# The second block's products as pairs of f32 halves on unsplit weights, on one Trainium2 core

## Chip, core and metric

The kernel runs on one core of a Trainium2 chip. The metric is device microseconds of one execution; the time before is the median of three runs. All matmuls run on TensorE (PE), which multiplies 128 rows of stationary weights (loaded by PEld) with up to 512 moving columns and writes to PSUM. VectorE is DVE, ScalarE is ACT, GpSimd is POOL, SyncE is SP. The trace gives one profiled execution, in us from the span's start.

## What is computed

Two transformer blocks on 512 tokens of width 1024, all in float32. The first (attention over tokens and context, then 32 routed experts, twice) is left alone by the change. The second, cut to its products:

```
h = rmsnorm(x, pre_mix_g)
z = h @ w_in                                  # 1024 x 7696
y_gla = gla_branch(...)                       # gated linear attention
y_sc  = sc_b * causal_dwconv(sc_c * sc_x)     # short convolution
y_dil = dilated_branch(d_q, d_k, d_v, pos)    # strided window attention
proj  = einsum('bsgc,gcd->bsgd', [y_gla, y_sc, y_dil], w_branch)
gates = sigmoid(h @ w_gate + b_gate)
x = x + rmsnorm(sum(gates * proj) @ w_mix_out, post_mix_g)
h = rmsnorm(x, pre_ffn_g)
gt = causal_dwconv(h @ w_ff_gate) + ff_conv_b  # 1024 x 2816
x = x + rmsnorm((gelu(gt) * (h @ w_ff_up)) @ w_ff_down, post_ffn_g)
```

## The kernel before

`second` (L1723) makes a plan of 92 weight tiles, nearly all 1 MB, in the order in which they are used, and a `Stream` (L34) loads them from HBM into slots. `ws.get()` splits the next tile: ACT writes `wh`, the weights rounded to fp32r (a reduced f32), and DVE (POOL in a few places) writes the rest, `wl = raw - wh`. The tokens `hTh`/`hTl`, the branch results `yh`/`yl`, `mTh`/`mTl` and `uTh`/`uTl` are split alike by `split` (L232). `mm3` (L226) then makes one product of three fp32r matmuls, high*high, high*low and low*high. Two raw slots are held, with pairs of split tiles behind them.

`proj_T` (L1763) takes a block of 128 weight columns as the stationary operand and moves 512 tokens: 8 products for 1024 rows. `proj` (L1770) takes 128 tokens as the stationary operand and moves 256 weight columns; in `dilated` the tokens of two of three groups are every fourth token. `out_rows` (L1915) takes 128 tokens and moves 512 columns, over 8 blocks of rows for `w_mix_out` and 22 for `w_ff_down`, each for four blocks of tokens and two halves of the width.

`second_body` (L1776) goes through the stages in order: the end of the first block and its norm (`front`, `back`, with `V`), `gla` with `short_conv` as filler, `dilated` with the projections of the next head as filler, gates and branch projections (`pm`, `pb`), the first `out_rows` with the norm of the feed-forward (`then`, which goes over `turned`), gate and up, the second `out_rows`. Within these, small f32 products stand in `gla` (`pg` L2086, `pe` L2063 in fp32r, `po`) and in `dilated` (`s` L2224, `po` L2250). A scheduler sets the order of instructions within a stage; each engine's queue runs in that order.

The experts of the first block, which the change leaves alone, hold products of 64 stationary columns: `up` (L1548) and `down` (L1572) take 64 tokens as weights and send two column ranges of the moving tile into the two halves of the PSUM partitions. The lines that matter there:

```
for i in range(2):
    for k in range(KC):                      # KC = 8
        for n in range(2):
            nc.tensor.matmul(pu[c][i][64 * n:64 * n + 64], xs[:, k, tok], w[:, k % 4, n * 256:(n + 1) * 256], ...)
```

`down` has four k and two n, with 512 columns each.

Of the kernel before, what the change touches and what calls it, by code (L numbers as in the profile page):

```python
# [23 lines left out]
P = 128  # L24
# [146 lines left out]
class Kern:  # L171
# [1542 lines left out]
    def turned(self, n, b, hT, pt):  # L1714

        for k0 in (0, 4):
# [46 lines left out]
    def proj_T(self, w, c, m=P):  # L1763

        pm = self.ps.tile([P, 512], F32, tag="mm", name="pm")
        for k in range(KC):
            self.mm3(pm[:m], w[0][:, k, c:c + m], w[1][:, k, c:c + m], self.hTh[:, k], self.hTl[:, k], k == 0, k == KC - 1)
        return pm

    def proj(self, w, tok, pm, c=0):  # L1770

        n = w[0].shape[2]
        for k in range(KC):
            self.mm3(pm[:, c:c + n], self.hTh[:, k, tok], self.hTl[:, k, tok], w[0][:, k], w[1][:, k], k == 0, k == KC - 1)

    def second_body(self):  # L1776
        nc, tc, A = self.nc, self.tc, self.A
        ws, proj_T = self.ws, self.proj_T
        with ExitStack() as es:
# [4 lines left out]
            self.hTh = hTh = hp.tile([P, KC, 512], FR, tag="hh", name="hTh")  # L1784
            self.hTl = hTl = hp.tile([P, KC, 512], FR, tag="hl", name="hTl")
            V = hp.tile([P, 4, 512], F32, name="V")
            with tc.tile_pool(name="sbx", bufs=2) as xp:
                second = []
                for b in range(4):
# [3 lines left out]
                    if b == 0:  # L1793
# [3 lines left out]
                        nc.gpsimd.dma_start(g, self.bcast_rows(A["pre_mix_g_2"], D))  # L1797
                gb = self.res[:, 4:6]
# [10 lines left out]
                Ws = [ws.get(0, sub=nc.gpsimd) for _ in range(2)]  # L1809

                def back(b, n):
                    self.turned(n, b, (hTh, hTl), lambda: ps.tile([P, 4, P], F32, tag="aux", name="pt"))
# [5 lines left out]
                for _ in piped(4, front, back, 2):  # L1818
                    pass
            self.res_stack.close()  # L1820

            def y_tiles(name):
                pool = ent(tc.tile_pool(name=name, bufs=1, side="right"))
                return tuple(pool.tile([P, 4, 512], FR, name=f"y{x}") for x in "hl")
# [3 lines left out]
            with ExitStack() as fs:  # L1828
                gla = self.gla(V, *y[0], ps)
                next(gla)  # L1830
                sp = fs.enter_context(tc.tile_pool(name="scp", bufs=2, side="right"))
                both(gla, self.short_conv(*y[1], sp))
            y.append(y_tiles("sby2"))
            self.dilated(*y[2], ps)

            mp = ent(tc.tile_pool(name="sbm", bufs=1, side="right"))
            mTh = mp.tile([P, KC, 512], FR, name="mTh")
            mTl = mp.tile([P, KC, 512], FR, name="mTl")
            bg = mp.tile([P, 24], F32, name="bg")
            nc.sync.dma_start(bg, A["b_gate_2"][0].rearrange("(k p) -> p k", p=P))  # L1840
            with tc.tile_pool(name="sbg", bufs=2) as gp:
                for d0 in range(0, 8, 2):
                    acc = gp.tile([P, 2, 512], F32, tag="acc", name="acc")
                    for g in range(3):
                        gts = []
                        wg = ws.get()
# [5 lines left out]
                        wh, wl = ws.get()  # L1852
                        for i in range(2):
                            pb = ps.tile([P, 512], F32, tag="mm", name="pb")
                            d = slice(i * P, (i + 1) * P)
                            for k in range(4):
                                self.mm3(pb, wh[:, k, d], wl[:, k, d], y[g][0][:, k], y[g][1][:, k], k == 0, k == 3)
# [3 lines left out]
                            else:  # L1861
                                nc.vector.tensor_mul(gt, gt, pb)
                                nc.vector.tensor_add(acc[:, i], acc[:, i], gt)
                            if g == 2:
                                self.split(mTh[:, d0 + i], mTl[:, d0 + i], acc[:, i])
# [4 lines left out]
            self.hTh = hTh = hp.tile([P, KC, 512], FR, name="hTh")  # L1870
            self.hTl = hTl = hp.tile([P, KC, 512], FR, name="hTl")
# [4 lines left out]
            with tc.tile_pool(name="sbmx", bufs=2) as xp:  # L1876
# [3 lines left out]
                def then(x, b, pt):  # L1880
                    self.turned(self.rms_apply(x, g, xp), b, (hTh, hTl), pt)

                self.out_rows(lambda k: (mTh[:, k], mTl[:, k]), KC, "post_mix_g_2", self.x_d, xp, then)
        with ExitStack() as es:
            ent = es.enter_context
            up = ent(tc.tile_pool(name="sfu", bufs=1, side="right"))
            uTh = up.tile([P, 22, 512], FR, name="uTh")
            uTl = up.tile([P, 22, 512], FR, name="uTl")
            with h2, tc.tile_pool(name="sfps", bufs=4, space=PSUM) as self.ps:
                with tc.tile_pool(name="sfg", bufs=2) as gp:  # L1890
                    for c0 in range(0, 22, 2):
                        ts = []
                        wg = ws.get(sub=None if c0 else nc.gpsimd)
# [12 lines left out]
                        wu = ws.get()  # L1906
                        for i in range(2):
                            t = ts[i]
                            pu = proj_T(wu, i * P)
                            nc.vector.tensor_mul(t, t, pu)  # L1910
                            self.split(uTh[:, c0 + i], uTl[:, c0 + i], t)
            with tc.tile_pool(name="sfx", bufs=2) as xp:
                self.out_rows(lambda k: (uTh[:, k], uTl[:, k]), 22, "post_ffn_g_2", A["out"], xp)

    def out_rows(self, lhs, kc, gname, dst, xp, then=None):  # L1915
# [6 lines left out]
        with tc.tile_pool(name="orps", bufs=1, space=PSUM) as ps:  # L1922
            pm = [ps.tile([P, 2, 512], F32, name=f"acc{b}", tag=f"acc{b}") for b in range(4)]

            def block(b, k0, w):
                tok = slice(b * P, (b + 1) * P)
                for i in range(2):
                    k = k0 + i
                    h, l = lhs(k)
                    for n in range(2):  # L1930
                        c = slice(n * 512, (n + 1) * 512)
                        self.mm3(pm[b][:, n], h[:, tok], l[:, tok], w[0][:, i, c], w[1][:, i, c], k == 0, k == kc - 1)

            for k0 in range(0, kc - 4, 2):
                w = self.ws.get()
                for b in range(4):
                    block(b, k0, w)
            w = [self.ws.get(), self.ws.get(ahead=0)]
            for b in range(4):
# [9 lines left out]
                if then and b:  # L1949
                    self.after(then, x, b - 1, ps)  # L1950
            if then:
# [6 lines left out]
    def short_conv(self, yTh, yTl, sp):  # L1958
# [5 lines left out]
        for i0 in (0, 2):  # L1964
            us, ts = [], []
            wb = ws.get()
# [5 lines left out]
            wc = ws.get()  # L1972
# [6 lines left out]
            wx = ws.get()  # L1979
            for i in range(2):  # L1980
# [7 lines left out]
                nc.vector.tensor_mul(t, t, v)  # L1988
                self.split(yTh[:, i0 + i], yTl[:, i0 + i], t)
                yield  # L1990

    def token_major(self, out, func, ps):

        for n in range(2):
            w = self.ws.get()
# [6 lines left out]
    def gla(self, V, yTh, yTl, ps):  # L2002
# [3 lines left out]
        with ExitStack() as es:  # L2006
# [4 lines left out]
            M = gp.tile([P, 9, P], FR, name="M")  # L2011
            mf = gp.tile([P, 9, P], F32, tag="mf", name="mf")
            nc.sync.dma_start(mf, A["k_gla_m"])
            nc.scalar.activation(M, mf, AF.Copy)
            mask = gp.tile([P, 8, P], F32, tag="mf", name="mask")
# [11 lines left out]
            for i in range(4):  # L2027
                if i % 2 == 0:
                    w = ws.get()
                nc.scalar.activation(qkT[:, i], proj_T(w, i % 2 * P), AF.Copy, scale=0.125 if i < 2 else 1.0)  # L2030
            aT = gp.tile([16, 512], F32, name="aT")
            nc.scalar.activation(aT, proj_T(ws.get(), 0, m=16)[:16], AF.Copy)

            lah = gp.tile([P, 4, 256], FR, name="lah")
# [323 lines left out]
```

## Time and profile before

| | |
|---|---|
| median of three runs | 3473.0 us (3469.5 to 3478.71) |
| the profiled execution | 3476.67 us, span 3474.9 us |
| PE busy | 3146.0 us (91%), 19045 instructions |
| PEld busy | 2289.0 us (66%) |
| DVE, ACT, POOL busy | 1479.0, 1038.0, 546.3 us |
| second block, from its first transposes | about 2285 to 3475 us |

Busy time counts the union of a group's rows, and a matmul's row includes its way through the array, so rows of one group overlap. The cost of a matmul in a stream is the distance between starts. Two of the experts' stages (about 660 to 1200 and 1800 to 2230 us) are the places where DMA is full.

### The profile page before, as it was taken

The page shows a single profiled execution, that of the slowest core. Times are in us where ns is not written, and L with a number is a line of the kernel's source. Part 1 is how long each engine was busy: PE and PEld are TensorE (multiplying, and loading weights), DVE is VectorE, ACT ScalarE, POOL GpSimd, SP SyncE. Part 2 cuts the span into 40 slices and gives each one's busy share as a digit, 9 for nine tenths or more (in the row PEclk, how much of TensorE's full clock was granted, in tenths as well). Part 3 has the DMA queues.
Part 4 walks back from the last instruction along what each step waited for, and adds up shares of the span by engine and source line. Part 5 has one row for each costly group of instructions (what it writes and reads, how often), then busy time and mean ns, then how long its engine had stood idle before and what let it go on. Part 6 is the DMA issues. An engine that isn't in the chain of part 4 may idle for free. (4 is left out here: it accounts for less than half of the span.)

```text
span 3474.9 us, 50552 instructions
## 1 busy us (share of the span) xinstructions
PE 3146.0 (91%) x19045; PEld 2289.0 (66%) x19045; DVE 1479.0 (43%) x3317; ACT 1038.0 (30%) x2243; POOL 546.3 (16%) x533
## 2 busy tenths in 40 slices
PE   7999999799999938999799999569999999979998
PEld 3677767555555526887655555258798888858887
DVE  5578665521111147655622112154533333365533
ACT  4355562111111114655211111023223332233321
POOL 1101002141211111011232121220022210010000
PEclk9999999799999978999899999879999999989999
DMA  7433142699999641111499999552121212423332
GB/s 249 153 98 108 53 155 98 278 398 416 416 416 415 274 135 49 30 54 55 168 381 366 399 416 402 230 157 73 54 75 49 67 55 91 148 77 97 97 127 73
DMA packets 273506, 647.72 MB, mean 186 GB/s; under 512 B 58210, under 2 KB 176370, under 8 KB 223042
## 3 DMA queue, kind: packets, MB, share of 16 engines
q1 hardware_dynamic: 245522, 602.04, 46.5%
q0 software_dynamic: 26608, 38.36, 3.6%
q8 instruction: 187, 3.06, 0.4%
q10 hardware_dynamic: 1088, 3.42, 0.3%
q14 instruction: 101, 0.83, 0.1%
HBM read 670.51 MB, written 47.61 MB: 207 GB/s over the span
## 5 line engine op out<-in xcount | busy, mean ns | idle before, releaser
L1555 PE MATMUL u<-raw,xs 128*64 128x256 f32 x5376 | 602.1, 383 | 4.5 <-DMA raw<-in_k_w 4.1
L1555 PEld LDWEIGHTS u<-raw,xs 128*64 128x64 f32 x5376 | 381.9, 138 | 205.7 <-issue 15.0
L235 DVE TENSOR_TENSOR wl<-raw,wh 128x2048 fp32r<-128x2048 f32 (+4 forms) x176 | 273.7, 1561 | 430.1 <-ACT wh L234 428.6
L234 ACT ACTIVATE wh<-raw 128x2048 fp32r<-128x2048 f32 (+3 forms) x180 | 239.4, 1335 | 436.6 <-PE pm L229 187.9
L228 PE MATMUL pm<-hTh,wh 128*128 128x512 f32 x872 | 344.2, 395 | 1.9 <-DVE hTl L235 1.4
L230 PE MATMUL pm<-hTh,wl 128*128 128x512 f32 x872 | 340.9, 391 | 1.1 <-DVE wl L235 1.1
L229 PE MATMUL pm<-hTl,wh 128*128 128x512 f32 x872 | 341.2, 391 | 0.0
L1575 PE MATMUL y<-raw,gs 128*64 128x512 f32 x1344 | 305.0, 600 | 4.6 <-ACT gs L1570 2.1
L1560 DVE TENSOR_TENSOR sg<-sg,u 128x256 f32<-128x256 f32 x132 | 55.0, 420 | 498.5 <-PEq L1608 263.2
L1590 POOL DMA_INDIRECT y_d<-ys,rt_si x128 | 127.4, 995 | 716.9 <-issue 274.9
L228 PE MATMUL pm<-wh,aTh 128*128 128x384 f32 (+2 forms) x576 | 206.9, 360 | 8.0 <-ACT aTh L444 8.0
L230 PE MATMUL pm<-wh,aTl 128*128 128x384 f32 (+2 forms) x576 | 203.3, 353 | 4.0 <-POOL aTl L445 3.6
L1575 PEld LDWEIGHTS y<-raw,gs 128*64 128x64 f32 x1344 | 91.3, 137 | 171.8 <-issue 162.1
L229 PE MATMUL pm<-wl,aTh 128*128 128x384 f32 (+2 forms) x576 | 201.1, 350 | 2.1 <-DVE wl L235 2.1
L1559 ACT ACTIVATE sg<-u 128x256 f32<-128x256 f32 x132 | 50.6, 383 | 469.4 <-PE u L1555 298.0
L228 PEld LDWEIGHTS pm<-hTh,wh 128*128 128x128 f32 x872 | 163.6, 188 | 37.5 <-DVE hTl L235 1.8
L230 PEld LDWEIGHTS pm<-hTh,wl 128*128 128x128 f32 x872 | 163.3, 187 | 36.1 <-DVE wl L235 1.5
L229 PEld LDWEIGHTS pm<-hTl,wh 128*128 128x128 f32 x872 | 163.6, 188 | 34.4
L258 PE MATMUL t<-ident,p 128*128 128x128 f32 x704 | 127.5, 288 | 6.2 <-DVE p L672 1.1
L228 PEld LDWEIGHTS pm<-wh,aTh 128*128 128x128 f32 x576 | 115.4, 200 | 18.1 <-ACT aTh L444 11.2
L230 PEld LDWEIGHTS pm<-wh,aTl 128*128 128x128 f32 x576 | 115.0, 200 | 12.0 <-issue 4.9
L1582 DVE SCALAR_TENSOR_TENSOR ys<-y,rt_sw,gate 128x512 f32<-128x512 f32 x64 | 46.6, 749 | 178.2 <-PE y L1575 91.2
(557 smaller groups left out, 5583.9 us busy)
## 6 DMA issues: line engine op xcount, KB each, us to landing
raw<-in_k_w SPq DMA_DIRECT2D x408, 1024.0 KB
raw<-in_mod_w SPq DMA_DIRECT2D x192, 256.0 KB
raw<-in_w_in SPq DMA_DIRECT2D x16, 1024.0 KB
raw<-in_w_in SPq DMA_DIRECT2D x24, 512.0 KB
raw<-in_w_gate SPq DMA_DIRECT2D x12, 1024.0 KB
raw<-in_w_ff_gate SPq DMA_DIRECT2D x11, 1024.0 KB
raw<-in_w_ff_up SPq DMA_DIRECT2D x11, 1024.0 KB
raw<-in_w_ff_down SPq DMA_DIRECT2D x11, 1024.0 KB
```

Of the source, the lines that this page charges most:

```text
L228: nc.tensor.matmul(out, lh, rh, start=start, stop=False)
L229: nc.tensor.matmul(out, lh, rl, start=False, stop=False)
L230: nc.tensor.matmul(out, ll, rh, start=False, stop=stop)
L234: self.nc.scalar.activation(h, x, AF.Copy)
L235: (sub or self.nc.vector).tensor_sub(l, x, h)
L258: self.nc.tensor.transpose(out, in_, self.ident[:k, :k])
L1555: nc.tensor.matmul(pu[c][i][64 * n:64 * n + 64], xs[:, k, tok], w[:, k % 4, n * 256:(n + 1) * 256], start=k == 0, stop=k == KC - 1)
L1559: nc.scalar.activation(sg[c], pu[c][0], AF.Silu)
L1560: nc.vector.tensor_mul(sg[c], sg[c], pu[c][1])
L1575: nc.tensor.matmul(py[c][64 * n:64 * n + 64], gs[:, c, k % 2, k // 2], W[k // 2][:, k % 2, n * 512:(n + 1) * 512], start=k == 0, stop=k == 3)
L1582: nc.vector.scalar_tensor_tensor(y, py[c], sw, gate, op0=OP.mult, op1=OP.mult)
L1590: nc.gpsimd.indirect_dma_start(out=y_rows, out_offset=bass.IndirectOffsetOnAxis(ap=si, axis=0), in_=y, in_offset=None, bounds_check=4 * nt ...
```

## The change

`mm` makes a product as f32 matmuls on 64 stationary columns each, into the matching half of the PSUM partitions, and takes the place of `mm3` in the whole second block, and of the small f32 products there. The weights are used as loaded (`ws.plain()`, `ws.take()`), the tokens and intermediate results are held once, in f32. The memory of the split pairs becomes four more slots for weights, six in all. In `gla` the products of the two row halves are interleaved, so both `pg` tiles are written at once.

```diff
+    def mm(self, out, l, r, start, stop):
+        m = l.shape[1]
+        for c in range(0, m, 64):
+            c = slice(c, min(m, c + 64))
+            self.nc.tensor.matmul(out[c], l[:, c], r, start=start, stop=stop)
...
     def turned(self, n, b, hT, pt):
...
-            self.split(hT[0][:, k0:k0 + 4, tok], hT[1][:, k0:k0 + 4, tok], t)
+            if k0:
+                nc.vector.tensor_copy(hT[:, k0:k0 + 4, tok], t)
+            else:
+                nc.scalar.activation(hT[:, k0:k0 + 4, tok], t, AF.Copy)
...
         for k in range(KC):
-            self.mm3(pm[:m], w[0][:, k, c:c + m], w[1][:, k, c:c + m], self.hTh[:, k], self.hTl[:, k], k == 0, k == KC - 1)
+            self.mm(pm[:m], w[:, k, c:c + m], self.hT[:, k], k == 0, k == KC - 1)
...
+                ws.more(ws.pool, 4)
...
-                Ws = [ws.get(0, sub=nc.gpsimd) for _ in range(2)]
+                Ws = ws.take(2)
...
-                        wg = ws.get(sub=None if c0 else nc.gpsimd)
+                        wg = ws.plain()
...
-                        nc.tensor.matmul(pe, lah[:, b, c], m, start=True, stop=False)
-                        nc.tensor.matmul(pe, lal[:, b, c], m, start=False, stop=True)
+                        self.mm(pe, las[:, b, c], m, True, True)
...
+                    pg = [ps.tile([P, 512], F32, tag="aux", name="pg") for _ in range(2)]
+                    for b in range(4):
+                        t = slice(b * P, (b + 1) * P)
+                        for hh in range(2):
+                            d = slice(hh * 64, (hh + 1) * 64)
+                            self.mm(pg[hh][:, t], ls[d, t], rs[d, t], True, True)
                     for hh in range(2):
-                        d = slice(hh * 64, (hh + 1) * 64)
-                        pg = ps.tile([P, 512], F32, tag="aux", name="pg")
-                        for b in range(4):
-                            t = slice(b * P, (b + 1) * P)
-                            nc.tensor.matmul(pg[:, t], ls[d, t], rs[d, t], start=True, stop=True)
                         nc.vector.copy_predicated(ST[:, 2 * pr + hh], mask[:, l:l + 1].bitcast(I32).to_broadcast([P, 4, P]),
-                                                  blk(pg))
+                                                  blk(pg[hh]))
```

The order on PE where the gates give way to the first branch projections (`hTh`, `hTl` or `hT` are the tokens, `yh`, `yl` or `y` a branch result, `wh` and `wl` the split weights, `raw` a weight tile as loaded; x16 is sixteen calls in a row; lines of the changed kernel are some seven higher). Before:

```order
L230 MATMUL pm<-hTh,wl 128x512
L228 MATMUL pm<-hTh,wh 128x512
L229 MATMUL pm<-hTl,wh 128x512
L230 MATMUL pm<-hTh,wl 128x512
L228 MATMUL pb<-yh,wh 128x512
L229 MATMUL pb<-yl,wh 128x512
L230 MATMUL pb<-yh,wl 128x512
```

After, with the buffers' numbers:

```order
L237 MATMUL pm_30075<-hT_26756,raw1_26765 64x512 x16
L237 MATMUL pb_30095<-y_27152,raw2_26779 64x512 x8
L237 MATMUL pb_30105<-y_27152,raw2_26779 64x512 x8
L237 MATMUL pm_30116<-hT_26756,raw3_26780 64x512 x16
L237 MATMUL pm_30135<-hT_26756,raw3_26780 64x512 x16
L237 MATMUL pb_30155<-y_27156,raw4_26781 64x512 x8
```

Three calls of 128 columns for each block of 128 rows become two of 64, so a `pm` tile of 24 calls has 16 now, and a `pb` tile of 12 has 8.

On PE at the first levels of `gla` (`pg` holds scores of one row half, `Pl` the scaled queries and keys of one level). Before:

```order
L230 MATMUL pm_27727<-hTh_26756,wl_27529 128x512
L2086 MATMUL pg_27757<-Pl_27754 128x128 x4
L2086 MATMUL pg_27763<-Pl_27754 128x128 x4
L2086 MATMUL pg_27772<-Pl_27769 128x128 x4
L228 MATMUL pm_27791<-hTh_26756,wh_27670 128x512
L229 MATMUL pm_27791<-hTl_26757,wh_27670 128x512
```

After:

```order
L237 MATMUL pg_27523<-Pl_27520 64x128 x2
L237 MATMUL pg_27524<-Pl_27520 64x128 x2
L237 MATMUL pm_27569<-hT_26756,raw2_26779 64x512
L237 MATMUL pg_27546<-Pl_27543 64x128 x3
L237 MATMUL pg_27547<-Pl_27543 64x128 x2
```

The two tiles of a level are filled in turns, and one call of a projection now stands between the two levels of a step.

On SP at the start of the second block (`y_d` holds the experts' results, `x_d` the tokens put aside, the rest are constants). Before:

```order
L1681 DMA y<-y_d 128x1024 x4
L1963 DMA cw<-in_sc_conv_w 128x4x1 x3
L1806 DMA x_d<-res 128x1024
L73 DMA raw_26765<-in_w_in 128x8x256
L73 DMA raw_26766<-in_w_in 128x8x256
L1806 DMA x_d<-res 128x1024 x3
```

After:

```order
L1688 DMA y<-y_d 128x1024 x4
L73 DMA raw_26779<-in_w_in 128x8x256
L73 DMA raw_26780<-in_w_in 128x8x256
L73 DMA raw_26781<-in_w_in 128x8x16
L73 DMA raw_26782<-in_w_in 128x8x256
L1817 DMA x_d<-res 128x1024 x4
```

Four weight loads stand directly behind the `y` loads now, ahead of the first `x_d` store.

## Rows read from the trace of the kernel before

**Rows 1.** Windows by stage: stretch, length, each engine's busy us (instructions), clock, DMA, GB/s.

```profile
2285.00:2832.90 547.90, 530.57 (x2824) 459.21 (x2824) 230.84 (x387) 181.10 (x264) 86.89 (x59) 0.99 0.22 63
2832.90:3020.60 187.70, 187.67 (x816) 153.13 (x816) 69.07 (x67) 52.59 (x53) 0.00 (x0) 1.00 0.31 96
3058.00:3099.30 41.30, 16.14 (x65) 11.98 (x63) 36.67 (x80) 14.78 (x22) 13.83 (x6) 0.67 0.29 102
3099.30:3340.50 241.20, 241.13 (x1056) 199.18 (x1056) 119.38 (x129) 78.69 (x88) 1.98 (x20) 0.99 0.29 92
3341.20:3465.00 123.80, 123.69 (x528) 99.37 (x528) 33.54 (x45) 22.13 (x17) 5.27 (x3) 1.00 0.27 98
...
2260.00:2270.00 10.00, 0.00 (x0) 0.00 (x0) 6.74 (x16) 1.91 (x1) 0.80 (x1) 0.50 1.03 359
```

**Rows 2.** Groups of PE by form, second block: line, tiles, shapes, count, busy, mean.

```profile
L228 PE MATMUL pm<-hTh,wh 128*128 128x512 f32 x864 | 341.1, 395 | 1.9 <-DVE hTl L235 1.4 <-ACT wh L234 0.5
L228 PE MATMUL pm<-wh,hTh 128*128 128x256 f32 x320 | 107.5, 336 | 1.6 <-ACT hTh L234 0.9 <-ACT V L2197 0.7
...
L2086 PE MATMUL pg<-Pl 64*128 64x128 f32 x224 | 26.4, 285 | 1.7 <-DVE ST L2087 1.7
```

**Rows 3.** PE rows of lines 1555 and 1575, the experts: duration least/median/most in ns.

```profile
L1555 PE MATMUL u<-raw,xs x5376: 379/379/689, 666.4 to 2220.0; 128*64 128x256 f32 x200
...
L1575 PE MATMUL y<-raw,gs x1344: 592/592/1061, 685.3 to 2232.9; 128*64 128x512 f32 x192
```

**Rows 4.** Timeline of PE in the experts: start, length, line, tiles, rows merged.

```profile
676.90 7.13 PE L1555 MATMUL u<-raw,xs 128*64 128x256 f32 x64
...
685.33 3.65 PE L1575 MATMUL y<-raw,gs 128*64 128x512 f32 x16
```

**Rows 5.** Timeline of PE at one score block of `dilated`.

```profile
2613.30 1.02 PE L2224 MATMUL s<-qk 128*128 128x512 f32 x2
2614.15 1.09 PE L2226 MATMUL s<-qk 128*128 128x128 f32 x4
2614.89 0.59 PE L228 MATMUL pm<-hTh,wh 128*128 128x512 f32 x1
2615.31 0.40 PE L229 MATMUL pm<-hTl,wh 128*128 128x512 f32 x1
2615.55 0.39 PE L230 MATMUL pm<-hTh,wl 128*128 128x512 f32 x1
```

**Rows 6.** Timeline of PE, products of 256 columns: contiguous tokens, then strided ones.

```profile
2305.03 0.28 PE L228 MATMUL pm<-wh,hTh 128*128 128x256 f32 x1
2305.15 0.28 PE L229 MATMUL pm<-wl,hTh 128*128 128x256 f32 x1
...
2710.10 0.40 PE L229 MATMUL pm<-wl,hTh 128*128 128x256 f32 x1
2710.33 0.40 PE L230 MATMUL pm<-wh,hTl 128*128 128x256 f32 x1
```

**Rows 7.** Groups of DVE by form, second block: the copies out of `pg`.

```profile
L2087 DVE COPY_PREDICATED ST<-mask,pg 128x512 f32<-128x512 int32 x32 | 22.8, 733 | 29.6 <-PE pg L2086 24.8 <-issue 4.9
```

**Rows 8.** Timeline of PE in the first block, half-width products, then full-width ones.

```profile
426.37 0.87 PE L729 MATMUL po<-pT,V 128*64 128x128 f32 x6
427.17 0.38 PE L455 MATMUL s<-QK 128*128 128x256 f32 x1
```

**Rows 9.** Timeline of DVE and POOL between the halves of the second block.

```profile
3071.74 8.97 POOL L235 TENSOR_TENSOR wl<-raw,wh 128x2048 fp32r<-128x2048 f32 x2
3071.85 4.43 DVE L249 SCALAR_TENSOR_TENSOR rs_t<-rs_y,rs_m 128x1 f32<-128x1 f32 x1
3076.31 4.42 DVE L253 SCALAR_TENSOR_TENSOR rs_y<-rs_t,rs_y 128x1 f32<-128x1 f32 x1
3080.76 0.22 DVE L249 SCALAR_TENSOR_TENSOR rs_t<-rs_y,rs_m 128x1 f32<-128x1 f32 x1
```

**Rows 10.** Timeline of DVE and POOL at the start of the second block.

```profile
2262.04 1.23 DVE L1802 TENSOR_TENSOR res<-res,y 128x1024 f32<-128x1024 f32 x1 [23.62 <-DMA y<-y_d]
...
2269.20 8.96 POOL L235 TENSOR_TENSOR wl<-raw,wh 128x2048 fp32r<-128x2048 f32 x2 [9.54 <-ACT wh L234]
2274.33 4.91 DVE L1802 TENSOR_TENSOR res<-res,y 128x1024 f32<-128x1024 f32 x1 [0.47 <-DMA res<-y_d]
```

More of the change, by code (lines that the diff above doesn't have):

```diff
@@ L1783, in second_body @@
             self.ps = ps = hs.enter_context(tc.tile_pool(name="sbps", bufs=2, space=PSUM))
-            self.hTh = hTh = hp.tile([P, KC, 512], FR, tag="hh", name="hTh")
-            self.hTl = hTl = hp.tile([P, KC, 512], FR, tag="hl", name="hTl")
+            self.hT = hT = hp.tile([P, KC, 512], F32, name="hT")
             V = hp.tile([P, 4, 512], F32, name="V")
@@ L1819, in second_body @@
                     pass
+                ws.free()
             self.res_stack.close()
@@ L1823, in y_tiles @@
                 pool = ent(tc.tile_pool(name=name, bufs=1, side="right"))
-                return tuple(pool.tile([P, 4, 512], FR, name=f"y{x}") for x in "hl")
+                return pool.tile([P, 4, 512], F32, name="y")
             y = [y_tiles("sby0")]
@@ L1828, in second_body @@
             with ExitStack() as fs:
-                gla = self.gla(V, *y[0], ps)
+                gla = self.gla(V, y[0], ps)
                 next(gla)
                 sp = fs.enter_context(tc.tile_pool(name="scp", bufs=2, side="right"))
-                both(gla, self.short_conv(*y[1], sp))
+                both(gla, self.short_conv(y[1], sp))
             y.append(y_tiles("sby2"))
-            self.dilated(*y[2], ps)
+            self.dilated(y[2], ps)
             mp = ent(tc.tile_pool(name="sbm", bufs=1, side="right"))
-            mTh = mp.tile([P, KC, 512], FR, name="mTh")
-            mTl = mp.tile([P, KC, 512], FR, name="mTl")
+            mT = mp.tile([P, KC, 512], F32, name="mT")
             bg = mp.tile([P, 24], F32, name="bg")
@@ L1869, in second_body @@
             hp = h2.enter_context(tc.tile_pool(name="sfh", bufs=1))
-            self.hTh = hTh = hp.tile([P, KC, 512], FR, name="hTh")
-            self.hTl = hTl = hp.tile([P, KC, 512], FR, name="hTl")
+            self.hT = hT = hp.tile([P, KC, 512], F32, name="hT")
             cw = hp.tile([P, 22, 4], F32, name="cw")
@@ L1880, in then @@
                 def then(x, b, pt):
-                    self.turned(self.rms_apply(x, g, xp), b, (hTh, hTl), pt)
-                self.out_rows(lambda k: (mTh[:, k], mTl[:, k]), KC, "post_mix_g_2", self.x_d, xp, then)
+                    self.turned(self.rms_apply(x, g, xp), b, hT, pt)
+                self.out_rows(mT, KC, "post_mix_g_2", self.x_d, xp, then)
         with ExitStack() as es:
@@ L1950, in out_rows @@
                     self.after(then, x, b - 1, ps)
+            self.ws.free()
             if then:
@@ L2010, in gla @@
             EX = gp.tile([P, 9, 4, P], F32, tag="EX", name="EX0")
[L2011 to L2015, printed above, removed]
+            M = gp.tile([P, 9, P], F32, name="M")
+            nc.sync.dma_start(M, A["k_gla_m"])
+            mask = gp.tile([P, 8, P], F32, name="mask")
             nc.sync.dma_start(mask, A["k_gla_mask"])
@@ L2039, in gla @@
                 for i in range(2):
-                    nc.tensor.matmul(pa[:, i], aT[:, (b + i) * P:(b + i + 1) * P], wa, start=True, stop=True)
+                    self.mm(pa[:, i], aT[:, (b + i) * P:(b + i + 1) * P], wa, True, True)
                 nc.vector.tensor_add(la[:, b:b + 2], pa, ba[:, None, :].to_broadcast([P, 2, 256]))
@@ L2108, in gla @@
                     out = po[:, h % 2, pr * P:(pr + 1) * P]
-                    nc.tensor.matmul(out, ST[:, h, b], V[:, b, h * P:(h + 1) * P], start=True, stop=b == 0)
+                    self.mm(out, ST[:, h, b], V[:, b, h * P:(h + 1) * P], True, b == 0)
                     if b:
-                        nc.tensor.matmul(out, qkT[d, pr, t], st[d, pr], start=False, stop=True)
+                        self.mm(out, qkT[d, pr, t], st[d, pr], False, True)
                 for i in range(2):
@@ L2249, in values @@
                         v = (V[:, 0, j] if j < 4 else V[:, j - 3, r])[:, h % 2 * P:h % 2 * P + P]
-                        nc.tensor.matmul(po[:, :P], v, pT[:, j], start=j == 0, stop=j == 5)
-                    self.split(yTh[:, h, tok], yTl[:, h, tok], po[:, :P])
+                        self.mm(po[:, :P], v, pT[:, j], j == 0, j == 5)
+                    nc.scalar.activation(yT[:, h, tok], po[:, :P], AF.Copy)
                 p = scores(0)
```

74 lines of the change are left out of this document (33 added, 41 removed).

## Prediction

> **What bounds the kernel now.** The change touches only the last third of the program, so I read the windows by stage first. From 2285 to 3465 us TensorE (PE) is busy nearly without a break: 530.6 of 547.9 us in the branches, 187.7 of 187.7 in the gates and branch projections, 241.1 of 241.2 in the feed-forward's first half, 123.7 of 123.8 in its second [rows 1]. One stretch is not PE's: 3058 to 3099 us, 16.1 of 41.3 us busy, where the rows are normalised between the two halves of the block [rows 1]. The clock is 0.99 to 1.00 in the full stretches, and weights never come late there: the DMA share is 0.22 to 0.31 in the long ones. So the second block's time is the number of products times the spacing of their starts, plus some 50 us in which DVE leads. The reader should look at spacings, not at the duration of one matmul: an fp32r product of 512 columns lasts 0.39 us in its row, but 816 of them fill 187.7 us, which is 0.230 us each.
>
> The list of PE groups by form gives the shapes [rows 2]. I call a *unit* one 128x128 block of weights or tokens times its moving rows. There are 1208 units that move 512 columns: 872 from `hT` (864 and 8 of 16 columns), 96 branch projections, and from the loops of `out_rows` 64 and 176. There are 320 units that move 256 columns. Each is three fp32r matmuls now.
>
> **Units of 512 columns: the term that decides.** Before: 187.7 us / 272 units = 0.690 us, 241.2 / 352 = 0.685, 123.8 / 176 = 0.703 [rows 1]; I take 0.69. After, a unit is two f32 calls of 64 columns. The trace of before has this very form in the experts, 64 stationary columns into each half of the PSUM partitions. One call of `up` asks for 2*8*2 = 32 products, but 64 rows stand in the trace: an f32 product is two instructions. The 64 take 7.13 us; without the tail of one (0.379 us less the 0.21 that 256 columns take, which is what 512 columns last longer: 0.592 - 0.379; so 0.17), 6.96 us / 16 pairs = 0.435 us for a pair of halves with 256 columns. `down` has 16 instructions of 512 columns in 3.65 us: (3.65 - 0.17) / 4 = 0.87 us a pair [rows 3, 4]. The two agree (2 * 0.435). An f32 row of 256 columns lasts as long as an fp32r row of 512, so each instruction goes over its columns twice: 0.21 us. The four of a pair would take 0.85 us one after the other and take 0.435, so the halves do run side by side. But all that a pair does is the work of one full-width f32 product, and that costs the same: the 128x512 scores of `dilated` are two instructions, and the next product starts 0.85 us after the first [rows 5]. So an unsplit f32 unit takes four passes whether whole or in halves, and three passes of fp32r are replaced by four.
> 1208 * (0.87 - 0.69) = +217 us. Bounds: 0.85 (the full-width row), +193; 0.91 (3.65 / 4, the short run with its tail), +266. I take 0.87, from the long run. The weight loads don't add: they ran beside the products in the same rows.
>
> **Units of 256 columns.** Contiguous tokens as weights: starts 0.12 us apart, 0.36 a unit. In the strided groups of `dilated` (every fourth token) starts are 0.23 apart, 0.70 a unit [rows 6]. That is 192 * 0.36 + 128 * 0.70 = 159 us. After: 320 * 0.435 = 139 us, so -20. The strided loads are the unknown here; if they stay the limit at half the width, 4 * 0.117 = 0.47 a unit, +5. Of the 64 units of `V`, three quarters stand under DVE's chain at the start and their growth (0.075 each) is hidden: -4.
>
> **Small products.** `pe` goes from two fp32r matmuls to a pair of f32 halves of 384 columns: 24 * (0.65 - 0.35) = +7 (three quarters of 0.87, and of twice 0.23). `po`, `s` and `pa` are f32 already and cost the same in halves, by the argument above. `pg` (256 f32 rows of 64x128, 224 of which take 26 us [rows 2]) is now interleaved over the two row halves and the two column halves; its floor is half, -13. Against that, both `pg` buffers are filled at once, so the second level of each two waits for two copies of 0.73 us [rows 7], where the first copy ran beside the second product before: eight times some 1.5 us, +12. PE's queue is in order, so the projections behind wait too. I take +6 for the group, from -13 to +12.
> Switching: after an f32 product the second fp32r start came 0.42 us after the first and not 0.23 [rows 5]. The built program has 76 places where fp32r follows f32; all go, some -8 to -14. In exchange transposes stay full width among halves, 62 changes of width. A 128x128 product came 0.80 us after six half-width ones had begun, 0.20 after the last of them, which start 0.12 apart, (0.87 - 0.27) / 5 [rows 8]: 0.08 more, 62 * 0.08 = +5. I take -4. (The Trainium skill, TensorEngine Tiling, Key Properties, says that a change of tiling mode drains TensorE. By a drain of the whole tail of 0.17 us it would be +11, and the group +2; the row's 0.08 agrees in kind.)
>
> **Splits and slots.** 92 weight splits on ACT with DVE or POOL, and the splits of `hT`, `y`, `mT`, `uT`, go. PE waits for almost none of them in the full stretches, so they are worth nothing there. Two places differ. Between the halves POOL splits two weights (8.97 us), and DVE's two smallest operations, 0.22 us elsewhere, last 4.43 and 4.42 us just under it, on the way to the next products [rows 9]. Without the two POOL rows: -8, and -2 for DVE's own `hTl`. What is late next there is DVE's normalising itself. At the start POOL's splits (8.96 us) stretch one addition of DVE to 4.91 us, where the first took 1.23 [rows 10]: -4. But the six slots put three more weights (3 MB) on SP's queue behind the `y` loads, and the 16 DMA engines are already full there (359 GB/s, share 1.03 [rows 1]) with the accumulating reads that DVE's chain waits for: 0 to 8 us, I take +4. Behind SP's later weight loads stand `x_d` stores and constants, which nobody needs soon.
>
> **Sum.** 217 - 20 - 4 + 7 + 6 - 4 - 10 - 4 + 4 = +192 us on an execution of 3476.7 us (span 3474.9): 3669. That execution is 3.7 us above the median of 3473.0, so I say 3666.
>
> **Rivals.** *Halves on one moving operand don't overlap.* In the experts the halves share their weights and move different columns; here they have different weights and read the same rows. If equal reads excluded each other, a pair would be 1.71 us, 1208 * 0.84 more, some 4680 us. Against it: both experts' halves also read one tile, at the same partitions, at once. Chance 0.04.
> *A pair costs half of what I read,* so the kernel gets faster. Mechanism: the 64-row runs of the experts would have to be held up by something else (the branches, full DMA), and a free pair would take 0.435 at 512 columns. Then 1208 * (0.435 - 0.69) = -308, the 256-column units -89, the rest -5: some 3070 us. It decides from a unit of 0.71 us down, since the other terms sum to -25. Against it: a run of 64 has no gap, two forms give the same price per column, and the full-width f32 row away from all DMA load gives it as well. (The Trainium skill, TensorEngine Tiling, Theoretical Speedup, gives up to 2x for 64 columns or fewer; that is against a half alone, and the rows above already contain it.) Chance 0.05.
> *Relief elsewhere outweighs the price.* All of PE's idle time between 2285 and 3465 is some 43 us [rows 1]; were it all to go, the time would still be some 3630. So this only moves the low end. Chance of a result within 0.3% by any mixture: 0.01.
> *The prefetch doesn't keep up* on six slots: a weight of 1 MB now serves 16 units, 14 us, at a load that the windows put under a third; not a case of its own.
>
> **How the numbers follow.** Forecast 0.90, rivals 0.04, 0.05, 0.01. Low end: units at 0.85 (-24) and the small terms at their good ends (-17): 3625. High end: strided loads (+5), no gain in `pg` and a full startup collision (+10), and units at 0.89, half way to 0.91 (+24): 3705. The far rivals lie outside. A measurement of this kernel can tell about 0.3%, 10 us, from no change: slower by more 0.94, within 0.01, faster by more 0.05.
>
> **What would show it.** In the changed kernel's rows: 8 instructions of 64 columns in 1.74 us in the feed-forward; its first half 3099-3340 grown from 241 to some 306 us, its second from 124 to 153, the gates and projections from 188 to 237; the clock at 1.00; the gap between the halves near 31 us; the strided units at 0.44 to 0.47. The forecast is wrong if the pair's spacing is not 0.85 to 0.91, or if PE shows idle time in those three stretches.

## The result, and the profile after

The changed kernel takes **3660.3 us** (median of 4 runs, 3658.7 to 3662.2), the kernel before 3472.1 in the same comparison. The ratio is **1.054, interval 1.052 to 1.056**: slower. The forecast was 3666, range 3625 to 3705.

Windows by stage of the changed kernel (columns as in [rows 1]): branches, gates and branch projections, the two parts of the stretch between the halves, feed-forward gate and up, feed-forward down.

```profile
2320.00:2877.40 557.40, 551.83 (x3838) 282.09 (x3836) 128.74 (x245) 112.81 (x208) 70.90 (x58) 1.00 0.20 57
2877.40:3112.50 235.10, 234.49 (x1092) 78.29 (x1088) 26.65 (x39) 15.80 (x23) 0.00 (x0) 1.00 0.27 83
3112.70:3155.00 42.30, 42.26 (x198) 14.28 (x200) 3.61 (x12) 1.84 (x3) 2.36 (x1) 1.00 0.52 150
3155.00:3192.90 37.90, 23.17 (x94) 9.36 (x88) 26.26 (x82) 9.60 (x18) 4.84 (x4) 0.74 0.32 111
3192.90:3497.60 304.70, 304.58 (x1408) 99.29 (x1408) 59.51 (x87) 28.29 (x45) 2.00 (x20) 0.99 0.23 73
3498.30:3649.70 151.40, 151.29 (x704) 50.48 (x704) 8.74 (x33) 3.34 (x6) 7.03 (x3) 1.00 0.19 66
```

Beside [rows 1]: 187.7 became 235.1, 241.2 became 304.7, 123.8 became 151.4. PE is as full as before, the clock as high, and DVE, ACT and the loads of weights have become much lighter. A unit costs 235.1 / 272 = 0.865 us, 304.7 / 352 = 0.865, 151.4 / 176 = 0.860, where it was 0.685 to 0.703.

Groups of PE by form, second block of the changed kernel (columns as in [rows 2]; each call is two rows):

```profile
L237 PE MATMUL pm<-hT,raw 128*64 128x512 f32 x3456 | 787.3, 594 | 0.9 <-DVE hT L1730 0.9
...
L237 PE MATMUL pm<-raw,hT 128*64 128x256 f32 x1280 | 149.9, 387 | 6.5 <-DVE hT L1730 6.0 <-ACT hT L1732 0.5
...
L237 PE MATMUL pg<-Pl 64*64 64x128 f32 x448 | 18.4, 277 | 0.0
```

The first group is the price: three groups of 864 rows, one start every 230 ns, have become 3456 rows, one start every 216. Two kinds of products became clearly cheaper: `pg`, 26.4 to 18.4 us [rows 2], and the strided units of 256 columns, 0.70 us [rows 6] to 0.44 a unit. Such units in the changed kernel:

```profile
2703.48 7.25 PE L237 MATMUL pm<-raw,hT 128*64 128x256 f32 x63
```

Stage by stage, in us of the profiled executions, before and after: up to the first product of 512 columns, 4.1 less, of which 3.4 are experts that ended earlier by scatter; branches 509.3 to 558.0; gates and branch projections with their tail 188.6 to 235.3; mixing and normalising 77.8 to 80.2; feed-forward 242.0 to 305.5 and 123.9 to 151.3. With 0.4 less behind the last product, and but for rounding, the sum is +184.0, the difference of the two spans.

### The profile page after: what moved, and what is told of

Its sections match the earlier page's. It is cut to its first block, busy times and chain, and to the rows that moved or that the text cites. A ratio compares the mean times of both kernels' runs of the same rounds, so it can differ in the third digit from the quotient of the medians.

```text
span 3658.9 us, 54508 instructions
## 1 busy us (share of the span) xinstructions
PE 3351.5 (92%) x21213; PEld 1891.7 (52%) x21213; DVE 1246.8 (34%) x3166; ACT 855.1 (23%) x2106; POOL 513.5 (14%) x529
## 5 line engine op out<-in xcount | busy, mean ns | idle before, releaser
L237 PE MATMUL pm<-hT,raw 128*64 128x512 f32 x3472 | 794.3, 594 | 0.9 <-DVE hT L1730 0.9
L237 PEld LDWEIGHTS pm<-hT,raw 128*64 128x64 f32 x3472 | 257.0, 137 | 485.7 <-issue 483.0
L237 PE MATMUL pm<-raw,hT 128*64 128x256 f32 x1280 | 149.9, 387 | 6.5 <-DVE hT L1730 6.0
L237 PE MATMUL acc<-raw,uT 128*64 128x512 f32 x704 | 151.3, 592 | 0.9 <-DVE uT L1917 0.9
L237 PEld LDWEIGHTS pm<-raw,hT 128*64 128x64 f32 x1280 | 112.1, 162 | 39.0 <-DVE hT L1730 6.4
L229 PEld LDWEIGHTS pm<-wl,aTh 128*128 128x128 f32 x576 | 114.1, 198 | 9.8 <-issue 6.2
L265 PEld LDWEIGHTS t<-ident,p 128*128 128x128 f32 x704 | 78.5, 141 | 48.5 <-issue 16.8
L237 PEld LDWEIGHTS acc<-raw,uT 128*64 128x64 f32 x704 | 50.5, 137 | 101.7 <-issue 99.9
```

The lines of the kernel that those rows point to most:

```text
L237: self.nc.tensor.matmul(out[c], l[:, c], r, start=start, stop=stop)
L265: self.nc.tensor.transpose(out, in_, self.ident[:k, :k])
```

## The experiments

### Whole products instead of halves

```diff
-        for c in range(0, m, 64):
-            c = slice(c, min(m, c + 64))
+        for c in range(0, m, P):
+            c = slice(c, min(m, c + P))
```

> The changed kernel with its f32 products as one call over all 128 columns instead of two calls of 64; all else as in the changed kernel. Theory (an f32 unit is four passes, whole or in halves): a unit of 512 columns at 0.85 to 0.87 us, so the feed-forward's first half at 299 to 306 us (304.7 in halves), its second at 150 to 153, the gates at 231 to 237, the whole within 0.7% of 3660 us. Rival (the halves have a price of their own, such as a change of half at each instruction or a second load, and whole products would be cheaper): a unit of 0.80 us or less, the first half under 285 us, the whole under 3610. Rival on the other side (the halves gain something): a unit above 0.91, the whole above 3710.

Measured: 3638.9 us, ratio to the kernel before 1.048 (1.046 to 1.050). The chain of waits of this kernel (start, us, what):

```profile
3170.10 304.63 PE pm L237 x704
3474.82 0.70 DVE uT L1917
3475.57 145.68 PE acc L237 x339
```

In the long stages nothing changed: 304.6 us for gate and up, with half as many instructions. So a unit is four passes, whole or in halves; theory and number hold there. But the whole is 21 us faster: within the 0.7% that the theory allowed, at its lower end, and not by cheaper units. In the profiled runs 15.3 of it lie in the branches (558.0 to 542.6) and 2.6 between the halves; 4 more stand ahead of the branches, where the experts, which are the same in both, happened to end 5.8 us earlier. In the trace of the changed kernel, PE at the levels of `gla` (start, us, what, count):

```profile
2417.41 1.10 PE L237 MATMUL pg<-Pl 64*64 64x128 f32 x32
2418.44 1.07 PE L237 MATMUL pm<-hT,raw 128*64 128x512 f32 x2
2419.44 1.58 PE L237 MATMUL pg<-Pl 64*64 64x128 f32 x32
2420.95 7.08 PE L237 MATMUL pm<-hT,raw 128*64 128x512 f32 x30
2427.96 1.10 PE L237 MATMUL pg<-Pl 64*64 64x128 f32 x32
```

The same step with whole products:

```profile
2411.95 1.16 PE L237 MATMUL pg<-Pl 64*128 64x128 f32 x16
2413.04 1.12 PE L237 MATMUL pm<-hT,raw 128*128 128x512 f32 x2
2414.09 1.58 PE L237 MATMUL pg<-Pl 64*128 64x128 f32 x16
2415.61 6.28 PE L237 MATMUL pm<-hT,raw 128*128 128x512 f32 x14
2421.81 1.16 PE L237 MATMUL pg<-Pl 64*128 64x128 f32 x16
```

Both steps hold two levels and one projection of eight units. The two rows of `pm` between the levels are one call: a whole unit here, half a unit there. From the start of their line to that of the next it is 1.00 us for the half unit and 1.05 for the whole one. A half that stands alone takes as long as a whole unit, and its other half is paid again behind the second level: 10.55 us a step against 9.86. The pair is *torn*. In the changed kernel some 25 units of the branches are torn, 12 of them in `gla`, since the scheduler places calls, and a unit is two calls.

The small products themselves are not cheaper whole. A score of `dilated` in the whole run:

```profile
2645.57 1.95 PE L237 MATMUL s<-qk 128*128 128x512 f32 x6
2647.33 7.05 PE L237 MATMUL pm<-hT,raw 128*128 128x512 f32 x16
```

It takes 1.76 us. In the changed kernel a score runs among four rows of projections, which are worth one unit, and all take 2.63 us together, so 1.77 for the score. Between fp32r products it took 1.59 [rows 5].

### The halves apart

In gate and up alone, all products of one half, then those of the other:

```diff
+        for h in (0, 64):
             for k in range(KC):
-                self.mm(pm[:m], w[:, k, c:c + m], ...)
+                self.mm(pm[h:h + 64], w[:, k, c + h:c + h + 64], ...)
```

> The changed kernel with, in the feed-forward's gate and up products alone, all eight products of one half of the columns ahead of the eight of the other, instead of half by half in turn. Theory (an instruction goes twice over its columns, 0.43 us for 512, and only the two halves of the array run beside each other): a unit takes 1.71 to 1.75 us, that stage 602 to 616 us instead of 304.7, the whole some 3960. Rival (the spacing of starts, 0.216 us, is what an instruction costs, whichever half it goes to): the stage stays at 300 to 310 us and the whole at 3660.

Measured: 3821.3 us (one run); the stage takes 462.3. PE's loads of weights in this stage (a load stands ahead of each product):

```profile
3301.72 0.14 PEld L237 LDWEIGHTS pm<-hT,raw 128*64 128x64 f32 x1 [0.29 <-issue]
3302.15 0.19 PEld L237 LDWEIGHTS pm<-hT,raw 128*64 128x64 f32 x3 [0.29 <-issue]
3302.58 0.19 PEld L237 LDWEIGHTS pm<-hT,raw 128*64 128x64 f32 x2 [0.23 <-issue]
3303.01 0.19 PEld L237 LDWEIGHTS pm<-hT,raw 128*64 128x64 f32 x2 [0.24 <-issue]
3303.49 0.14 PEld L237 LDWEIGHTS pm<-hT,raw 128*64 128x64 f32 x1 [0.29 <-issue]
3303.92 0.14 PEld L237 LDWEIGHTS pm<-hT,raw 128*64 128x64 f32 x1 [0.29 <-issue]
```

Inside a run on one half an instruction starts every 0.43 us, as the theory has it: two passes over 512 columns. The rival (0.216 whichever half) falls. But at each change of half seven instructions go in three such steps: the first of the new half run beside the last of the old one. A run of 16 takes 462.3 / 88 = 5.25 us, not 16 * 0.43 = 6.9; 1.6 us, four instructions, overlap. So the 602 to 616 us that I expected were too high because I took the overlap for all or nothing: in this run halves ran beside each other where they stood within about four instructions of each other in PE's order.

### Two products instead of three

```diff
-        nc.tensor.matmul(out, lh, rl, start=False, stop=False)
+        if not self.two:
+            nc.tensor.matmul(out, lh, rl, start=False, stop=False)
```

> The kernel before with the second of the three fp32r products (high part by low part) left out in the feed-forward's two halves, whose result therefore lacks that part. Theory (time is passes over the columns, 0.23 us each): units at 0.46 us, the first half 161 to 164 us instead of 241, the second 82 to 84 instead of 124, the whole some 3352. Rival (the splits of the weights by ACT and DVE, 16 units apart, or the weights' transfers hold the stage near its old time): the first half above 180 us with PE waiting for DVE, ACT or DMA.

Measured: 3368.8 us (one run). Windows of the two halves of the feed-forward:

```profile
3101.10:3263.10 162.00, 162.00 (x704) 133.64 (x704) 115.03 (x129) 77.82 (x87) 1.99 (x20) 0.99 0.42 133
3268.00:3353.00 85.00, 85.00 (x352) 67.87 (x352) 29.54 (x37) 21.16 (x16) 3.35 (x2) 0.97 0.34 124
```

162.0 / 352 = 0.460 us a unit, two thirds of 0.685 [rows 1]: time follows the passes, and the splits (115 us of DVE and 78 of ACT in 162) don't hold it up. Against the expected total 17 us are missing: 4.9 us between the two halves instead of 0.7 (PE now waits 4.7 us for DVE there), 4 more behind the end, 2 ahead of the first, and 3 in the second, at a clock of 0.97; the other 4 are that the profiled run of the kernel before, from which the stages were taken, lies 4 us above its median.

### Three slots instead of six

```diff
-                ws.more(ws.pool, 4)
+                ws.more(ws.pool, 1)
```

> The changed kernel with three slots for weights instead of six. Theory (a weight serves 14 us of products at a fifth of the DMA engines, the slots are worth nothing but 3 MB more at the start): the whole within 0.3% of the changed kernel's 3660 us, at most 4 us less because the start has less to fetch. Rival (the six slots carry the unsplit products through late transfers): PE waits for weights in the branches and in the rows' normalising, 10 us or more above 3660.

Measured: 3659.7 us, ratio to before 1.054 (1.052 to 1.056), the same as the changed kernel. The six slots are worth nothing here, and the 3 MB that they add at the start cost nothing that can be seen: the first product of 512 columns came at 2320.9 us with three slots and at 2319.5 with six.

### The products `pg` by themselves

The kernel before, with `pg` alone changed, once as in the change (halves of the columns) and once only with the row halves in turn (the second is shown; in the first, an inner loop goes over the column halves too):

```diff
-                    for hh in range(2):
-                        pg = ps.tile(...)
-                        for b in range(4):
-                            nc.tensor.matmul(pg[:, t], ls[d, t], rs[d, t], ...)
+                    pg = [ps.tile(...) for _ in range(2)]
+                    for b in range(4):
+                        for hh in range(2):
+                            nc.tensor.matmul(pg[hh][:, t], ls[d, t], rs[d, t], ...)
```

> The kernel before with only the products pg changed: both heads' buffers first, then head by head in turn over the two halves of the rows, each product in two halves of the columns, as in the changed kernel. In the kernel before two levels take some 4.1 us of PE (1.6 and 2.5), in the changed kernel some 2.6. Theory (the two row halves run beside each other, and the copies that the second level waits for are no longer than what it gained): 8 to 13 us faster than the kernel before. Rival (my term as it stood in the prediction: the second level's wait for two copies outweighs the overlap): 6 us slower.

> The same with the products pg whole over the 128 columns: only the order over the two row halves is changed. If the turn of the row halves is the gain, 8 to 13 us faster than the kernel before, within 2 us of the run with halves of the columns. If the halves of the columns are needed for it, less than 4 us faster.

Measured: ratios 0.9973 (0.9962 to 0.9985) and 0.9966 (0.9951 to 0.9981), 9 and 12 us faster. From the first `pe` to the transposes of `O` the profiled runs give less, 132.6 us before, 127.3 and 125.5 here: 5.3 and 7.1. Both lie inside the intervals (0.9985 is 5.2 us, 0.9981 is 6.6), and the block's start came up to 11 us earlier or later in the profiled runs that share the code before it. So the gain is real, and it is the order over the row halves that brings it; the column halves add nothing that can be seen. The wait that I had feared, with halves of the columns (PE's waits from 2370 to 2480 us: total, times, longest):

```profile
PE pg L2088 <- DVE ST L2090: 3.1, 6, 0.6
```

and with whole columns:

```profile
PE pg L2088 <- DVE ST L2090: 0.6, 2, 0.3
```

Half a us a time, not 1.5: other products stand between the two levels in PE's order, and most of the two copies of 0.73 us [rows 7] runs beside them.

### No split on POOL between the halves

```diff
-                        wg = ws.get(sub=None if c0 else nc.gpsimd)
+                        wg = ws.get()
```

> The kernel before with the first two weight splits of the feed-forward on DVE instead of POOL. Theory (POOL's 8.97 us beside DVE stretch two tiny operations of DVE to 4.4 us on the way to the next products): those two back at about 0.2 us, of which DVE's own two splits of 2.3 us each may take some back: 4 to 8 us faster. Rival (DVE would have been late there without POOL, or its own splits take the place): within 2 us of the kernel before, or up to 5 us slower.

Measured: ratio 0.998 (0.9967 to 0.9993), 7 us faster. From the first product of the mixing to the first of `down`, 319.8 us became 315.3: 4.5. PE's waits there, 3000 to 3110 us:

```profile
PE t L258 <- DVE rm_s L1704: 9.5, 2, 5.2
PE t L258 <- DVE rs_t L249: 3.3, 1, 3.3
```

In the kernel before the first of these is 15.4 us, with a longest of 11.1, in the changed kernel 7.5. The two operations of 4.4 us [rows 9] are gone, one of 2.3 is left, and DVE's own two splits of 2.3 us take some of it back. The sign and the size are those expected.

### The strided projections turned round

The kernel before, with weights stationary and tokens moving for the two strided groups of `dilated`, then transposed:

```diff
+                    for c in range(2 if g else 0):
+                        pm = proj_T(w, c * P)
+                        nc.scalar.activation(vT.rearrange("p (r i) -> p i r", r=4),
+                                             pm.rearrange("p (i r) -> p i r", r=4), AF.Copy)
...
+                        for r in range(4):
+                            self.transpose(t[:, r], vT[:, r * P:(r + 1) * P])
+                        nc.scalar.activation(V[:, g, :, c * P:(c + 1) * P], t, AF.Copy)
```

> The kernel before with the strided projections of the dilated branch turned round: the weights are the stationary side and all 512 tokens the moving one (16 fp32r units of 512 columns per weight at 0.69 us), ACT writes the result in the order of the residues, and eight 128x128 transposes (about 0.2 us each) bring it to tokens by channels. Theory (every fourth token as stationary side holds a unit of 256 columns at 0.70 us instead of 0.36): four weights at 22.5 us become 11.0 + 1.6, so some 39 us faster, 30 at least. Rival (PE then waits for ACT's copy before the transposes, or the strided load was not what held the starts at 0.23 us): less than 20 us faster, with PE idle before the transposes.

Measured: 3433.2 us, ratio 0.9877 (0.9853 to 0.9900). From the transposes of `O` to the first `pb`, 322.7 us became 283.7: 39.0 less where 39 was expected. The added work, PE's and ACT's rows (least, median and most ns), and who waited for ACT's copies (us, times):

```profile
L258 PE MATMUL vt<-ident,vT x32: 270/272/328, 2520.6 to 2671.5; 128*128 128x128 f32 x32
L2197 ACT ACTIVATE vT<-pm x8: 1071/1095/1127, 2515.3 to 2670.0; 128x512 f32<-128x512 f32 x8
...
  PE vt L258: 0.9, 2
```

PE waits for the copies 0.9 us in all. So the strided stationary side did hold the fp32r starts at 0.23 us [rows 6]. It is also where the change gained, 0.70 to 0.44 us a unit, but hardly by its halves. The same strided products in the run with whole f32 products:

```profile
2688.26 7.64 PE L237 MATMUL pm<-raw,hT 128*128 128x256 f32 x32
```

That is a start every 0.234 us, as in fp32r, but two starts a unit instead of three, 0.47 us. The halves take off the last 0.02.

### Torn pairs mended

The changed kernel, in the branches alone:

```diff
         for k in range(KC):
+            if k == 0 and m == P and self.branches:
+                self.nc.tensor.matmul(pm, w[:, k, c:c + m], self.hT[:, k], start=True, stop=False)
+                continue
             self.mm(pm[:m], w[:, k, c:c + m], self.hT[:, k], k == 0, k == KC - 1)
```

> The changed kernel with one edit in the branches: of each projection of 512 columns the first of the eight units is one whole f32 call instead of two halves; all small products stay in halves. In the changed kernel the order puts a group of other products between the two halves of just this unit, some 22 times, and the half that stands alone takes 1.00 us, as long as a whole unit. Theory (a pair torn apart pays for its halves one after the other, 0.76 to 0.87 us more): 15 to 18 us off, less up to 7 us for some 80 more changes of width at 0.08, so 3643 to 3652 us. Rival (what the whole products of the first experiment gained lay in the small products, scores, masks and values): within 3 us of the changed kernel's 3660, or above it.

Measured: 3653.2 us, 7 below the changed kernel, one us outside the theory's range and 4 outside the rival's. The rows tell the two apart. PE at the same step of `gla`:

```profile
2420.80 1.10 PE L237 MATMUL pg<-Pl 64*64 64x128 f32 x32
2421.83 1.12 PE L1779 MATMUL pm<-hT,raw 128*128 128x512 f32 x2
2422.89 1.53 PE L237 MATMUL pg<-Pl 64*64 64x128 f32 x32
2424.35 6.23 PE L237 MATMUL pm<-hT,raw 128*64 128x512 f32 x28
2430.51 1.10 PE L237 MATMUL pg<-Pl 64*64 64x128 f32 x32
```

A step is 9.71 us, 0.84 less than torn, with `pg` still in halves: here it was the torn unit and not the small products. But where nothing was torn, a projection pays for its two changes of width:

```profile
2321.48 1.12 PE L1779 MATMUL pm<-hT,raw 128*128 128x512 f32 x2
2322.53 6.23 PE L237 MATMUL pm<-hT,raw 128*64 128x512 f32 x28
2328.69 1.12 PE L1779 MATMUL pm<-hT,raw 128*128 128x512 f32 x2
```

7.21 us instead of 8 * 0.864 = 6.91: 0.15 for each change of width, twice the 0.08 that I had read from [rows 8]. Over some 40 projections that takes back much of the gain. The branches came out at 552.5 us against 558.0: 1.3 more ahead of the first `pe`, 4.3 less from there to the transposes of `O`, 2.4 less in `dilated`.

### The parts that pay, together

The kernel before with the strided projections turned round, `pg` by row halves, no POOL split, and the queries of `dilated` in the order of the residues:

```diff
+                            oq, xq = o.rearrange("p (r i) -> p i r", r=4), lambda v: v.rearrange("p (i r) -> p i r", r=4)
+                            nc.vector.scalar_tensor_tensor(oq, xq(pm), sc, xq(cos), op0=OP.mult, op1=OP.mult)
...
-                    nc.tensor.matmul(s[:, 0:512], QK[0, 0][:, tok], QK[0, 1], start=True, stop=True)
+                    nc.tensor.matmul(s[:, 0:512], QK[0, 0][:, r * P:(r + 1) * P], QK[0, 1], start=True, stop=True)
```

> The kernel before with four edits: the strided projections turned round (43 us faster by itself), the products pg over the row halves in turn (10 to 12), no split on POOL in the feed-forward (7), and, new, the queries of the dilated branch written in the order of the residues, so that the scores' stationary side is contiguous. The last should save the strided load at four of a score's six instructions, 0.23 against 0.12 us, 0.44 us for each of 16 scores, 7 us. If the four add up: 3403 to 3412 us. If the queries' order only moves the wait to POOL's strided writes, 3412 to 3420.

Measured: **3419.0 us, ratio 0.985 (0.983 to 0.986)**, faster than both kernels, though not by all that was expected. By stages against the kernel before: 7.1 less in `gla`, 40.1 in `dilated`, 5.0 between the halves, 52 in all. The three known parts bring what their stages had shown. What is missing is the new part: `dilated` lost 1.1 us more than without it, not 7. PE's loads and the writers of the queries:

```profile
L2249 PEld LDWEIGHTS s<-qk x64: 186/190/209, 2563.9 to 2767.8; 128*128 128x128 f32 x64
...
L2230 DVE SCALAR_TENSOR_TENSOR qk<-pm,cos x12: 1066/1092/1122, 2537.8 to 2744.2; 128x512 f32<-128x512 f32 x12
L2235 POOL TENSOR_TENSOR qk<-qk,xs x12: 1549/1567/1844, 2539.3 to 2745.6; 128x512 f32<-128x512 f32 x12
```

The load did fall, from 308 to 190 ns, but a score went only from 1.59 to 1.57 us, and all scores together lost 1.7 us: most of the load had been hidden beside the f32 rows. I had taken 1.77 for a score from the run with whole f32 products around it. The strided writes lengthen DVE's and POOL's operations (0.69 to 1.09 and 1.29 to 1.57 us), but PE waits for POOL hardly longer (2.8 us instead of 2.7), so the rival has the total right and the cause wrong.

## Why the prediction held, and where it did not

**The deciding term was right.** Three fp32r passes against four f32 passes: the prediction had 0.87 us a unit, the stages show 0.865, 0.865 and 0.860. That it read 0.87 off a run of 16 rows in the experts is worth 1208 * 0.005 = 6 us, as much as 3666 stands above 3660; this is luck in part, since the small terms below are off by more and cancel (and the sum as written gives 3665). Gate and up came to 304.7 for 306 forecast, down to 151.4 for 153, gates to 235 for 237. The pass count is shown from both sides: two fp32r products give 0.460, whole f32 products the same 304.6. (The Trainium skill, FP8 and Floating Point Precision, TensorE Precision Notes, gives true FP32 four passes through the array; the trace agrees, 0.865 us against 0.230 for an fp32r product of the same shape, 3.8 times.)

**Both far rivals fell.** Halves on one moving operand do overlap: 0.216 us a start in turn, 0.43 apart. A pair at half the price was never there.

**The 256-column units** came at 0.111 us from start to start in the 63 strided rows above, 0.443 a unit, between the 0.435 taken and the bound of 0.47.

**The branches were right by two errors that cancel.** The prediction's prices give about +47 us there, and +48.6 was measured. Ahead of the first `pe` they give some +12 (40 units at 0.18, 64 small ones at 0.075), and 10.2 was measured. But from there to the transposes of `O` they give some +30 (96 units at 0.18, 20 small ones, `pe` 7, `pg` 6, less the switching) where 19.7 was measured, and from there to the gates some +5 (208 units at 0.18 and 44 small ones, less 128 strided at 0.265 and the switching) where 18.7 was. Step one at fault: **`pg`, +6**, was a gain; alone in the kernel before it is -5.3, because the wait for the copies is 0.5 us a time and not 1.5. Step two: **the units' calls were taken to stand side by side everywhere**, so that a torn unit had no term. The order printed ahead of the prediction shows one call of a projection alone between two levels of `pg`; that is half a unit, and I did not price it. In `gla` it costs 0.7 to 0.84 us a place. The whole-product run puts the net of all that halves cost and gain in the branches at 15.3 us, 6.9 of them before the transposes of `O` and 8.4 in `dilated`. That all of the 8.4 is torn units is not shown: whole first units brought 2.4 there. That `s` costs the same in halves as whole held (1.77 and 1.76 us), but a score costs 0.18 more than it did between fp32r products, some 3 us over 16 scores. This leaves some 6 us of gain before the transposes of `O` and some 2 us of growth in `dilated` that I can't assign.

**Between the halves** the -10 was about right: 64 units at +0.175 make +11.2, the stage grew by 2.4, so 8.8 came back; PE's wait for DVE's `rm_s` fell from 15.4 to 7.5 us. POOL's part of that is shown by the run without its split, 4.5 of the 8 that I gave it. The sign named for it, a gap near 31 us, is not met as it stands: the window that ends with the stage is 37.9 us where it was 41.3, but PE now works in 23.2 of them and not in 16.1, so its idle time fell from 25.2 to 14.7.

**At the start** the two terms of 4 us were meant to cancel, and the whole is about nothing: from the start of the experts' last product to the first of 512 columns it is 90.7 us before and 90.0 after. But only one term is there in full. The addition that POOL's splits had stretched to 4.91 us [rows 10], in the changed kernel:

```profile
2272.00 1.23 DVE L1813 TENSOR_TENSOR res<-res,y 128x1024 f32<-128x1024 f32 x1 [0.64 <-DMA res<-y_d]
```

Of the 4 us for the transfers about one can be seen, and not from the six slots: the chain's first addition starts 30.2 us after that product where it was 29.1, and with three slots 30.6. What happens behind it is larger than either term: the first transposes come 12 us sooner after the experts, and from them to the first product of 512 columns it takes 47.8 us instead of 36.2. No run shows what moved these two.

## What to carry to other kernels

Count passes before counting instructions: two half-width f32 calls are one full-width f32 product, four passes, and here only something that was empty before gained, as the two row halves of `pg` did when they were filled in turns. If work is cut into calls that pay only side by side, read in the built order whether they still stand side by side; a scheduler that places calls tears them, here for 0.4% of the time. And a strided stationary operand is worth a look in any fp32r kernel: turning those of the two strided groups round was worth 39 of 3473 us, more than anything else here. In f32 the same stride cost little, 0.47 against 0.43 us a unit of 256 columns.

## What the runs showed of the hardware

- Two column halves overlapped only where their instructions stood within about four of each other: runs of 16 on alternate halves took 5.25 us, not 6.9 and not 3.46. (The Trainium skill, TensorEngine Tiling, Key Properties, says that tiles run their loads and matmuls in parallel; here that held for neighbours in PE's order alone.)
- A change between 64 and 128 columns cost 0.15 us in the projections, where I had read 0.08 next to transposes [rows 8].
- Writing 512 f32 in the order of the residues, each element 128 behind the last one in groups of four, took ACT 1.10 us (0.61 for the contiguous `V<-vt`), DVE 1.09 (0.69) and POOL 1.57 (1.29).
- A stationary load of 128 columns, every fourth element, took 308 ns in f32 against 190 and 329 ns in fp32r against 192. Products of 256 columns then started every 0.233 us in fp32r against 0.120, and every 0.234 in whole f32 against 0.217; in f32 halves it was 0.111 against 0.107.
